# Latent attention scores: three products of 96 to 98 rows repacked into two of 128 rows and one of 34 rows that lies in another row half for each head of a pair

## The chip, the core and the metric

The kernel runs on one core of one Trainium2 chip. The metric is the device time of one execution in microseconds; the time before is the median of three runs. The engines are named as the profile names them: PE (TensorE, the matmuls; PEld is its weight load), DVE (VectorE), ACT (ScalarE), POOL (GpSimd) and SP (SyncE, which issues the DMAs).

## What is computed

A trunk of two layers works on 1024 latent tokens and 256 context tokens of width 1024. Layer 0 is attention with two head groups (8 grouped-query heads and 8 latent heads), layer 1 is recurrent. The change lies in the latent heads of layer 0. Cut from the reference:

```python
qa = (rms_norm(cq, q_norm_a) @ w_uq).reshape(bsz, t, MLA_HEADS, MLA_NOPE + MLA_ROPE)   # 64 + 32
kv = (rms_norm(ckv, kv_norm_a) @ w_ukv).reshape(bsz, t, MLA_HEADS, MLA_NOPE + MLA_V)   # 64 + 64
q_rope = apply_axial_rope(q_rope, rope_a); kr = apply_axial_rope(kr, rope_a)
qa = concatenate([q_nope, q_rope]); ka = concatenate([k_nope, broadcast_to(kr)])       # 96 each
sc = einsum('bqhgd,bkhd->bhgqk', qblk, k) * scale
p  = softmax(sc); o = einsum('bhgqk,bkhd->bqhgd', p, v)
```

Each head's key and query thus have 96 elements: 64 of its own, and 32 rotary ones, whose key part all heads share.

## The kernel before, in words

All matmuls of the scores take operands of the type float32r. To come near float32, every operand is split into a high part h and a low part l, and a product is the sum of three matmuls into one PSUM tile: hh, hl and lh.

`attention` (L594) is a generator that first runs beside the input projection and then alone. Its work is a list of 16 units: 8 of the grouped-query heads ("g"), then 8 of the latent heads ("m"). A unit is a pair of heads p and a part of the query tokens: S0 is 512 latent tokens and the 256 context tokens, S1 the other 512 latent tokens. A unit is worked off in steps `it`, one for each block of 128 keys: 10 steps for a segment of 512 queries, 2 for the 256 context queries (which see the context keys alone). So the latent heads have 4 x 2 x 10 steps of 512 columns and 4 x 2 steps of 256.

The main loop (L975) does for each step, in this order: `scores` of the next step (L792), `sums` of the step before (L830, softmax sums, on POOL and partly DVE), and after every second step `values` for both (L815, PSUM tile pv, 64 output columns for each of the two heads). `scores` computes 128 keys x 512 queries for head j = 0, then for j = 1, each in a PSUM tile "pb" of a ring of 3, and ACT takes exp of it into a tile "pt" of a ring of 11. For a latent head these are three matmuls (L808 to L810):

```python
self.mm(sp[:, :n], kh[0:98, ks], qh[0:98, j, o], True, False)
self.mm(sp[:, :n], kh[0:96, ks], ql[0:96, j, o], False, False)
self.mm(sp[:, :n], kl[0:96, ks], qh[0:96, j, o], False, True)
```

Rows 96 and 97 of kh are ones, those of qh the two bf16 terms of minus the row maximum.

Between the matmuls of `scores` the function `between` lets the generator `prep` of the next unit issue pieces: for a unit with base 0 first `prep_k_mla` (L688: three chunks of tokens, 256, 512 and 512; the key projection of both heads, split into kh and kl), then for all units `prep_q_mla` (L711: for each head and segment six projection matmuls, the rotary product with the table `tab` on DVE, and the split into qh and ql), then `prep_max` (L734: score matmuls of 128 queries against the keys in high parts alone, whose row maxima DVE takes, and the `bias` that writes them back as two rows). The PSUM tiles of `prep` ("ps") come from a ring of 4. Small work tiles "f" (L638, L722) are a ring of 3.

PE and DVE issue in the order in which the program is written there (a manual schedule, L943); ACT, POOL and SP in the order that a scheduler gives them. Every engine issues in its order.

The shared rotary part of the keys is made once in `project0` (`krb`, L396 to L430) and stored to DRAM as `d["kr"]`, 64 rows of high part (32 rows, then ones) and 64 rows of low part (32 rows, then zeros), from where `prep_k_mla` loads it under each head's 64 rows.

Of the kernel before, what the change touches and what calls it, by code (L numbers as in the profile page):

```python
# [17 lines left out]
P = 128  # L18
D = 1024
# [92 lines left out]
class Trunk:  # L112
# [202 lines left out]
    def project0(self, er, el, att):  # L315
# [84 lines left out]
        nc.gpsimd.tensor_copy(krb[:, :, 0, 96:128], one.rearrange("p (a b) -> p a b", a=4))  # L400

        def post_a(c):
# [15 lines left out]
            nc.gpsimd.tensor_copy(krb[:, :nt, 0, 64:96], kr)  # L418
# [175 lines left out]
    def attention(self, es):  # L594
# [12 lines left out]
        def kb_tile(first):  # L607
            return self.til(u0, [P, NTOK], F32R, "kb", bufs=2) if first else self.til(ap, [P, NTOK], F32R, "kb", bufs=6)
# [63 lines left out]
        def q_tiles(u):  # L672
            u["qh"], u["ql"] = (self.til(u0, [P, 2, 768], F32R, t, bufs=2) for t in ("qh", "ql"))
            return u["qh"], u["ql"]
# [13 lines left out]
        def prep_k_mla(u):  # L688
            p = u["p"]
            kh, kl = [], []  # L690
            for j in range(2):
                a, b = (kb_tile(p % 2 and j) for _ in range(2))
                nc.sync.dma_start(a.bitcast(F32)[64:128], d["kr"][0])
                nc.sync.dma_start(b.bitcast(F32)[64:96], d["kr"][1, 0:32])
                kh.append(a)
                kl.append(b)
            u["k"] = [(kh[0], kl[0]), (kh[1], kl[1])]
            wu, ck = M["wu"], M["ck"]
            ws = slice(p * P, (p + 1) * P)
            for t0, n in CH:  # L700
# [3 lines left out]
                nc.scalar.activation(kh[0][0:64, tk], acc[0:64, :n], AF.Copy)  # L704
                nc.vector.tensor_tensor(kl[0][0:64, tk], acc[0:64, :n], kh[0][0:64, tk], op=ALU.subtract)
                sc = self.til(ap, [P, 512], F32, "f", bufs=3)
                nc.scalar.copy(sc[0:64, :n], acc[64:128, :n])
                self.split(kh[1][0:64, tk], kl[1][0:64, tk], sc[0:64, :n], "v", "g")
                yield

        def prep_q_mla(u):  # L711
            qh, ql = q_tiles(u)
            wq, cq, tab = M["wq"], M["cq"], M["tab"]
            for j in range(2):
                h = 2 * u["p"] + j
                for t0, n in u["segs"]:
# [3 lines left out]
                    for k in range(2):  # L720
                        self.mm3(acc[:, :n], wq[:, k, 0, h], wq[:, k, 1, h], cq[:, k, 0, tk], cq[:, k, 1, tk], k == 0, k == 1)
                    qs = self.til(ap, [P, 512], F32, "f", bufs=3)  # L722
                    if t0 == 0:
                        nc.scalar.copy(qs[0:96, :n], acc[0:96, :n])
                    else:
                        lt = slice(t0 - NCTX, t0 - NCTX + n)
                        w = self.til(ap, [P, 512], F32, "f", bufs=3)
                        nc.vector.tensor_tensor(qs[0:96, :n], acc[0:96, :n], tab[0:96, lt], op=ALU.mult)
                        nc.vector.tensor_tensor(w[64:96, :n], acc[96:128, :n], tab[96:128, lt], op=ALU.mult)
                        nc.vector.tensor_tensor(qs[64:96, :n], qs[64:96, :n], w[64:96, :n], op=ALU.add)  # L730
                    self.split(qh[0:96, j, o], ql[0:96, j, o], qs[0:96, :n], "a", "g")
                    yield

        def prep_max(u):  # L734

            K, r0 = (P, 64) if u["kind"] == "g" else (96, 96)
            mt = u["ql"] if u["kind"] == "g" else u["qh"]
# [4 lines left out]
            def bias(j, t0, n):  # L742
                o = t0 - u["base"]
                pm = self.ps([P, 512])
                for i in range(n // P):
                    self.mm(pm[r0:r0 + 2, i * P:(i + 1) * P], nb[:, j, o // P + i, :], self.ident_bf, True, True)
                nc.scalar.activation(mt[r0:r0 + 2, j, o:o + n], pm[r0:r0 + 2, :n], AF.Copy)
# [44 lines left out]
        def scores(it):  # L792
# [6 lines left out]
            for j in range(2):  # L799
                if j:  # L800
                    yield
                sp = self.ps([P, 512], "pb")
                kh, kl = u["k"][j]
                if u["kind"] == "g":
                    self.mm(sp[:, :n], kh[:, ks], qh[:, j, o], True, False)
                    self.mm(sp[:, :n], kl[0:66, ks], ql[0:66, j, o], False, True)
                else:
                    self.mm(sp[:, :n], kh[0:98, ks], qh[0:98, j, o], True, False)  # L808
                    self.mm(sp[:, :n], kh[0:96, ks], ql[0:96, j, o], False, False)
                    self.mm(sp[:, :n], kl[0:96, ks], qh[0:96, j, o], False, True)  # L810
# [1430 lines left out]
```

## Time and profile before

| | |
|---|---|
| median of three runs | 1787.96 us (1785.87 to 1790.78) |
| the profiled execution, its own time | 1786.52 us |
| its span in the profile, first to last instruction | 1784.7 us |
| mean granted TensorE clock over the span | 0.960 of full speed |
| PE, PEld, DVE, ACT, POOL busy, share of the span | 91%, 67%, 66%, 42%, 45% |
| latent heads' steps, first and last score matmul | 608.8 us and 906.4 us after the span's start |

The profile has a page (busy shares, the span in slices, DMA queues, the chain that ended last, the costliest groups) and a trace that can be asked for a stretch. A matmul's shown duration contains its way through the array: matmuls overlap, so what one costs in a row of them is the distance from its start to the next start, not its duration. In a timeline, equal instructions that follow each other stand in one row with their count. An engine's idle time stands with what ended it.

### The profile page before, as it was taken

The numbers are of one execution on the slowest core, as the hardware profiler recorded it, in microseconds if no ns is written. First come the engines' busy times: TensorE is split into PE (matmuls) and PEld (weight loads), VectorE is DVE, ScalarE is ACT, GpSimd is POOL, SyncE is SP. The second block draws the span as 40 slices with busy tenths as digits, with TensorE's granted clock in tenths as the row PEclk, the third lists the DMA queues.
The fourth block names the chain that finished last, engine by engine and source line by source line (L and its number), as shares of the span: only waits on it lengthen the run. The fifth ranks groups of instructions, "written<-read, shape, count | busy, mean of one in ns | idle before, by whom it ended". The sixth has DMA issues, their size and how long they took to land.

```text
span 1784.7 us, 25505 instructions
## 1 busy us (share of the span) xinstructions
PE 1630.5 (91%) x9020; PEld 1195.9 (67%) x9020; DVE 1177.7 (66%) x2186; ACT 741.0 (42%) x1500; POOL 811.2 (45%) x727
## 2 busy tenths in 40 slices
PE   5999899989999999999899989988978995898996
PEld 2997766735555566666457876666856883798885
DVE  2657623247566857667847975889956894477787
ACT  2543401145545454444524344767643421233431
POOL 1432200067666678767643851332213794572131
PEclk9999999999999999999999999989989997899998
DMA  9243485164322101121333323333458538985543
GB/s 354 75 154 109 147 292 201 60 142 144 94 53 59 35 22 47 30 59 48 98 98 113 130 91 102 111 107 115 145 140 213 159 115 233 295 259 174 172 147 106
DMA packets 239931, 234.31 MB, mean 131 GB/s; under 512 B 61958, under 2 KB 188306, under 8 KB 237756
## 3 DMA queue, kind: packets, MB, share of 16 engines
q1 hardware_dynamic: 239804, 232.69, 42.8%
q8 instruction: 71, 1.16, 0.3%
q14 instruction: 56, 0.46, 0.1%
HBM read 162.97 MB, written 69.66 MB: 130 GB/s over the span
## 4 chain that ended last, share of the span: by engine, by line
PE 51%; DVE 18%; DMA 13%; issue 7%; ACT 6%; POOL 3%; SPq 2%; ACTq 0%; DVEq 0%; POOLq 0%
PE ps L88 34%; PE pb L88 10%; PE pv L88 7%; DMA wst<-in_att_w_in 2%; DVE f L88 2%; DMA wh<-in_rec_w_out 2%; DVE x L88 2%; DVE yc L88 2%; DVE lw L88 1%; DVE mx L88 1%; DMA qh<-d_q 1%; DMA d_xa<-WX 1%; DVE WX L88 1%; DVE r L88 1%; DVE lu L88 1%
## 5 line engine op out<-in xcount | busy, mean ns | idle before, releaser
L88 DVE TENSOR_REDUCE mx<-ps 128x1 f32<-128x512 f32 (+1 forms) x384 | 207.2, 593 | 155.8 <-PE ps L88 154.1
L88 POOL TENSOR_TENSOR accp<-accp,pt 128x512 f32<-128x512 f32 x202 | 266.0, 1338 | 62.0 <-ACT pt L88 60.4
L88 PE MATMUL ps<-h1h,wf 128*128 128x512 f32 (+1 forms) x864 | 270.5, 388 | 3.5 <-DVE tm L88 1.6
L88 ACT ACTIVATE pt<-pb 128x512 f32<-128x512 f32 (+1 forms) x352 | 194.2, 577 | 185.7 <-PE pb L88 178.0
L88 PE MATMUL pb<-qh,kb 96*128 96x512 f32 (+4 forms) x528 | 210.0, 412 | 5.2 <-ACT pt L88 4.6
L88 PEld LDWEIGHTS ps<-h1h,wf 128*128 128x128 f32 x864 | 161.1, 194 | 35.4 <-issue 3.7
L88 PE MATMUL ps<-h1l,wf 128*128 128x512 f32 (+1 forms) x432 | 163.7, 379 | 0.0
L88 PEld LDWEIGHTS pb<-qh,kb 128*128 128x128 f32 (+2 forms) x528 | 100.1, 191 | 92.6 <-issue 65.4
L88 PE MATMUL pb<-ql,kb 66*128 66x512 f32 (+3 forms) x352 | 137.5, 392 | 0.7 <-ACT ql L88 0.7
L88 PE MATMUL ps<-kb,qh 128*128 128x512 f32 (+3 forms) x416 | 121.7, 368 | 8.9 <-DVE mx L88 5.0
L88 POOL TENSOR_TENSOR accp<-pt,pt 128x512 f32<-128x512 f32 (+1 forms) x47 | 55.9, 1208 | 137.0 <-ACT pt L88 125.3
L88 PEld LDWEIGHTS ps<-kb,qh 128*128 128x128 f32 (+1 forms) x416 | 76.9, 191 | 44.8 <-DVE mx L88 12.8
L88 POOL TENSOR_TENSOR ml<-m,mh 128x512 fp32r<-128x512 f32 (+1 forms) x24 | 52.6, 2205 | 114.0 <-ACT mh L88 114.0
L88 DVE SCALAR_TENSOR_TENSOR yc<-xb,rT,yc 128x1283 f32<-128x1283 f32 (+1 forms) x48 | 84.1, 1759 | 24.5 <-ACT yc L88 24.1
L88 PEld LDWEIGHTS ps<-h1l,wf 128*128 128x128 f32 x432 | 83.9, 194 | 16.6 <-issue 3.6
L88 PE MATMUL ps<-w,mh 128*128 128x512 f32 x256 | 82.5, 404 | 3.4 <-ACT mh L88 3.4
L88 PE MATMUL pv<-pt,vm 128*64 128x512 f32 (+1 forms) x352 | 83.1, 586 | 1.6 <-DVE mo L88 1.6
L88 PE MATMUL pv<-pt,vgqa 128*64 128x512 f32 (+1 forms) x352 | 83.1, 593 | 1.0 <-DVE mo L88 1.0
L88 PE MATMUL ps<-wo,mh 128*128 128x512 f32 x256 | 82.1, 399 | 1.2 <-ACT mh L88 0.7
L88 PE MATMUL ps<-wh,hh 128*128 128x416 f32 (+2 forms) x240 | 82.8, 349 | 0.2 <-ACT hs L88 0.2
L88 PE MATMUL ps<-wh,hl 128*128 128x416 f32 (+2 forms) x240 | 81.7, 343 | 0.0
L88 PE MATMUL ps<-wl,hh 128*128 128x416 f32 (+2 forms) x240 | 81.5, 342 | 0.0
(373 smaller groups left out, 3706.0 us busy)
## 6 DMA issues: line engine op xcount, KB each, us to landing
modw<-in_mod_w SPq DMA_DIRECT2D x16, 1024.0 KB
wfs<-in_rec_w_in SPq DMA_DIRECT2D x22, 512.0 KB
modw<-in_mod_w SPq DMA_DIRECT2D x16, 512.0 KB
wst<-in_att_w_in SPq DMA_DIRECT2D x24, 256.0 KB
d_q<-qo SPq DMA_DIRECT2D x20, 256.0 KB
lx<-d_xl SPq DMA_DIRECT2D x8, 640.0 KB
d_w<-WX SPq DMA_DIRECT2D x20, 256.0 KB
W<-d_w SPq DMA_DIRECT2D x20, 256.0 KB
```

Source lines behind the costliest of these rows:

```text
L88: return fn(*args, **kw)
```

## The change

The same 290 products per query and key (98 + 96 + 96) are laid out as 128 + 128 + 34 rows. Of one head, the first matmul holds [kh of 64 rows; rotary kh; rotary kh] against [qh of 64; rotary qh; rotary ql]; the second holds kh and kl of the 64 rows against ql and qh, one above the other; the third holds 32 rows of the rotary kl and the two rows of ones against the rotary qh and the maximum. The third operand's keys ("kc") are loaded once for all heads, in rows 0 to 33 and again in rows 64 to 97; head 0 of a pair uses the upper half and head 1 the lower one, so the two third matmuls stand next to each other, in tiles of 64 rows. For that, `scores` opens the second head's PSUM tile before it ends the first's, and exp of the first head comes after the two.

Preparation: `prep_k_mla` makes four ACT copies and two DVE subtractions per chunk (before: two ACT copies, a DVE subtraction, a DVE cast, a POOL subtraction); `prep_q_mla` makes for a segment of 512 four ACT copies, four DVE operations and a POOL one (before: one, three, one), for the segment of 256 five ACT copies, one DVE and one POOL operation (before: two, none, one). Tiles: the ring pt goes from 11 to 10; the tiles of q have one buffer for S0 and one for S1 instead of a ring of two of equal size; the tiles of keys of even p get a pool of their own ("kx"), with the same reuse as before.

```diff
--- before.py
+++ after.py
@@ -397,7 +397,7 @@
         one = self.til(wka, [P, P], F32, "ones", bufs=1)
         nc.gpsimd.memset(one, 1.0)
         nc.gpsimd.memset(krb.bitcast(F32), 0.0)
-        nc.gpsimd.tensor_copy(krb[:, :, 0, 96:128], one.rearrange("p (a b) -> p a b", a=4))
+        nc.gpsimd.tensor_copy(krb[:, :, 1, 96:128], one.rearrange("p (a b) -> p a b", a=4))
 
         def post_a(c):
             t0, n = CH[c]
@@ -415,7 +415,7 @@
                     nc.gpsimd.tensor_tensor(s5(u)[:, :, :, h], s5(kr)[:, :, :, 1 - h], s5(sin32[:, tt])[:, :, :, h], op=ALU.mult)
                 nc.gpsimd.tensor_tensor(v, v, u, op=ALU.add)
                 kr = v
-            nc.gpsimd.tensor_copy(krb[:, :nt, 0, 64:96], kr)
+            nc.gpsimd.tensor_copy(krb[:, :nt, 0, 64:128].rearrange("p t (r e) -> p t r e", r=2), kr.unsqueeze(2).broadcast_to([P, nt, 2, 32]))
             nc.gpsimd.tensor_tensor(krb[:, :nt, 1, 64:96], kr, krb[:, :nt, 0, 64:96], op=ALU.subtract)
             for a, b, q in ((0, 256, 0), (256, 384, 4)):
                 nc.gpsimd.tensor_tensor(r[:, :nt, a:b], r[:, :nt, a:b], rs[:, q:q + nt].unsqueeze(2).broadcast_to([P, nt, b - a]), op=ALU.mult)
@@ -604,8 +604,10 @@
                 for segs in (S0, S1):
                     units.append(dict(kind=kind, p=p, segs=segs, f=p + (4 if kind == "g" else 0), base=min(x[0] for x in segs), i=len(units)))
 
-        def kb_tile(first):
-            return self.til(u0, [P, NTOK], F32R, "kb", bufs=2) if first else self.til(ap, [P, NTOK], F32R, "kb", bufs=6)
+        def kb_tile(first, even=False):
+            if even:
+                return self.til(kx, [P, NTOK], F32R, "kx", bufs=4)
+            return self.til(u0 if first else ap, [P, NTOK], F32R, "kb", bufs=2)
 
         gk = []
 
@@ -670,7 +672,8 @@
                 yield
 
         def q_tiles(u):
-            u["qh"], u["ql"] = (self.til(u0, [P, 2, 768], F32R, t, bufs=2) for t in ("qh", "ql"))
+            n = sum(x[1] for x in u["segs"])
+            u["qh"], u["ql"] = (self.til(u0, [P, 2, n], F32R, f"{t}{n}", bufs=1) for t in ("qh", "ql"))
             return u["qh"], u["ql"]
 
         def prep_q_gqa(u):
@@ -687,54 +690,66 @@
 
         def prep_k_mla(u):
             p = u["p"]
-            kh, kl = [], []
+            ka, kb = [], []
             for j in range(2):
-                a, b = (kb_tile(p % 2 and j) for _ in range(2))
+                a, b = (kb_tile(p % 2 and j, p % 2 == 0) for _ in range(2))
                 nc.sync.dma_start(a.bitcast(F32)[64:128], d["kr"][0])
-                nc.sync.dma_start(b.bitcast(F32)[64:96], d["kr"][1, 0:32])
-                kh.append(a)
-                kl.append(b)
-            u["k"] = [(kh[0], kl[0]), (kh[1], kl[1])]
+                ka.append(a)
+                kb.append(b)
+            u["k"] = [(ka[0], kb[0]), (ka[1], kb[1])]
+            if "kc" not in M:
+                kc = M["kc"] = self.til(ap, [P, NTOK], F32R, "kc", bufs=1)
+                for j in range(2):
+                    nc.sync.dma_start(kc.bitcast(F32)[64 * j:64 * j + 64], d["kr"][1])
             wu, ck = M["wu"], M["ck"]
             ws = slice(p * P, (p + 1) * P)
             for t0, n in CH:
                 acc = self.ps([P, 512])
                 tk = slice(t0, t0 + n)
                 self.mm3(acc[:, :n], wu[:, 0, 0, ws], wu[:, 0, 1, ws], ck[:, 0, tk], ck[:, 1, tk], True, True)
-                nc.scalar.activation(kh[0][0:64, tk], acc[0:64, :n], AF.Copy)
-                nc.vector.tensor_tensor(kl[0][0:64, tk], acc[0:64, :n], kh[0][0:64, tk], op=ALU.subtract)
-                sc = self.til(ap, [P, 512], F32, "f", bufs=3)
-                nc.scalar.copy(sc[0:64, :n], acc[64:128, :n])
-                self.split(kh[1][0:64, tk], kl[1][0:64, tk], sc[0:64, :n], "v", "g")
+                nc.scalar.activation(ka[0][0:64, tk], acc[0:64, :n], AF.Copy)
+                nc.vector.tensor_tensor(kb[0][64:128, tk], acc[0:64, :n], ka[0][0:64, tk], op=ALU.subtract)
+                nc.scalar.activation(kb[1][64:128, tk], acc[64:128, :n], AF.Copy)
+                nc.vector.tensor_tensor(kb[1][0:64, tk], acc[64:128, :n], kb[1][64:128, tk], op=ALU.subtract)
+                nc.scalar.activation(kb[0][0:64, tk], acc[0:64, :n], AF.Copy)
+                nc.scalar.activation(ka[1][0:64, tk], acc[64:128, :n], AF.Copy)
                 yield
 
         def prep_q_mla(u):
+
+
             qh, ql = q_tiles(u)
+            qc = u["qc"] = self.til(ap, [P, sum(x[1] for x in u["segs"])], F32R, f"qc{u['base'] // 768}", bufs=1)
             wq, cq, tab = M["wq"], M["cq"], M["tab"]
             for j in range(2):
                 h = 2 * u["p"] + j
+                bh, bl = (slice(64, 128), slice(0, 64)) if j == 0 else (slice(0, 64), slice(64, 128))
                 for t0, n in u["segs"]:
                     tk = slice(t0, t0 + n)
                     o = slice(t0 - u["base"], t0 - u["base"] + n)
                     acc = self.ps([P, 512])
                     for k in range(2):
                         self.mm3(acc[:, :n], wq[:, k, 0, h], wq[:, k, 1, h], cq[:, k, 0, tk], cq[:, k, 1, tk], k == 0, k == 1)
+                    nc.scalar.activation(qh[0:64, j, o], acc[0:64, :n], AF.Copy)
+                    nc.vector.tensor_tensor(ql[bl, j, o], acc[0:64, :n], qh[0:64, j, o], op=ALU.subtract)
+                    nc.scalar.activation(ql[bh, j, o], acc[0:64, :n], AF.Copy)
                     qs = self.til(ap, [P, 512], F32, "f", bufs=3)
                     if t0 == 0:
-                        nc.scalar.copy(qs[0:96, :n], acc[0:96, :n])
+                        nc.scalar.copy(qs[64:96, :n], acc[64:96, :n])
                     else:
                         lt = slice(t0 - NCTX, t0 - NCTX + n)
                         w = self.til(ap, [P, 512], F32, "f", bufs=3)
-                        nc.vector.tensor_tensor(qs[0:96, :n], acc[0:96, :n], tab[0:96, lt], op=ALU.mult)
+                        nc.vector.tensor_tensor(qs[64:96, :n], acc[64:96, :n], tab[64:96, lt], op=ALU.mult)
                         nc.vector.tensor_tensor(w[64:96, :n], acc[96:128, :n], tab[96:128, lt], op=ALU.mult)
                         nc.vector.tensor_tensor(qs[64:96, :n], qs[64:96, :n], w[64:96, :n], op=ALU.add)
-                    self.split(qh[0:96, j, o], ql[0:96, j, o], qs[0:96, :n], "a", "g")
+                    nc.scalar.activation(qh[64:96, j, o], qs[64:96, :n], AF.Copy)
+                    nc.gpsimd.tensor_tensor(qh[96:128, j, o], qs[64:96, :n], qh[64:96, j, o], op=ALU.subtract)
+                    nc.scalar.activation(qc[64 * j:64 * j + 32, o], qs[64:96, :n], AF.Copy)
                     yield
 
         def prep_max(u):
 
-            K, r0 = (P, 64) if u["kind"] == "g" else (96, 96)
-            mt = u["ql"] if u["kind"] == "g" else u["qh"]
+            K = P if u["kind"] == "g" else 96
             mx = self.til(u0, [P, 8, 3], F32, "mx", bufs=2)
             m8 = self.til(u0, [P, 2, 6, 2], F32, "m8", bufs=2)
             nb = self.til(u0, [P, 2, 6, 2], BF16, "nb", bufs=2)
@@ -742,9 +757,14 @@
             def bias(j, t0, n):
                 o = t0 - u["base"]
                 pm = self.ps([P, 512])
+                if u["kind"] == "g":
+                    r0, dst = 64, u["ql"][64:66, j, o:o + n]
+                else:
+                    r0 = 32 + 64 * j
+                    dst = u["qc"][r0:r0 + 2, o:o + n]
                 for i in range(n // P):
                     self.mm(pm[r0:r0 + 2, i * P:(i + 1) * P], nb[:, j, o // P + i, :], self.ident_bf, True, True)
-                nc.scalar.activation(mt[r0:r0 + 2, j, o:o + n], pm[r0:r0 + 2, :n], AF.Copy)
+                nc.scalar.activation(dst, pm[r0:r0 + 2, :n], AF.Copy)
 
             for t0, n in u["segs"]:
                 if t0 == 0:
@@ -796,21 +816,34 @@
             qh, ql = u["qh"], u["ql"]
             scale = 64 ** -0.5 if u["kind"] == "g" else 96 ** -0.5
             it["pt"] = []
-            for j in range(2):
-                if j:
-                    yield
-                sp = self.ps([P, 512], "pb")
-                kh, kl = u["k"][j]
-                if u["kind"] == "g":
+
+            def exp(sp):
+                pt = self.til(ap, [P, 512], F32, "pt", bufs=10)
+                nc.scalar.activation(pt[:, :n], sp[:, :n], AF.Exp, scale=scale)
+                it["pt"].append(pt)
+
+            if u["kind"] == "g":
+                for j in range(2):
+                    if j:
+                        yield
+                    sp = self.ps([P, 512], "pb")
+                    kh, kl = u["k"][j]
                     self.mm(sp[:, :n], kh[:, ks], qh[:, j, o], True, False)
                     self.mm(sp[:, :n], kl[0:66, ks], ql[0:66, j, o], False, True)
-                else:
-                    self.mm(sp[:, :n], kh[0:98, ks], qh[0:98, j, o], True, False)
-                    self.mm(sp[:, :n], kh[0:96, ks], ql[0:96, j, o], False, False)
-                    self.mm(sp[:, :n], kl[0:96, ks], qh[0:96, j, o], False, True)
-                pt = self.til(ap, [P, 512], F32, "pt", bufs=11)
-                nc.scalar.activation(pt[:, :n], sp[:, :n], AF.Exp, scale=scale)
-                it["pt"].append(pt)
+                    exp(sp)
+                return
+            kc, qc = M["kc"], u["qc"]
+            sp = self.ps([P, 512], "pb")
+            for k, q in zip(u["k"][0], (qh, ql)):
+                self.mm(sp[:, :n], k[:, ks], q[:, 0, o], q is qh, False)
+            yield
+            s1 = self.ps([P, 512], "pb")
+            self.mm(sp[:, :n], kc[0:34, ks], qc[0:34, o], False, True)
+            self.mm(s1[:, :n], kc[64:98, ks], qc[64:98, o], True, False)
+            exp(sp)
+            for k, q in zip(u["k"][1], (qh, ql)):
+                self.mm(s1[:, :n], k[:, ks], q[:, 1, o], False, q is ql)
+            exp(s1)
 
         def values(it):
             u, t0, n, kb, nkb = it["u"], it["t0"], it["n"], it["kb"], it["nkb"]
...
```

(Left out: the opening and closing of the pool "kx", and names of tiles that the end of the function reuses.)

How the order moves on PE, in the place of one step of 512 columns of the latent heads (pair p = 2, between the key projection and the first maxima; names: pb score tiles, qh/ql/qc query parts, kb/kx/kc key tiles). Before:

```order
L88 MATMUL pb_1732_7004<-qh_1599_6531,kb_1489_6126 128x512
L88 MATMUL pb_1732_7004<-ql_1600_6532,kb_1489_6126 128x512
L88 MATMUL pb_1732_7004<-qh_1599_6531,kb_1490_6127 128x512
L88 MATMUL pb_1734_7010<-qh_1599_6531,kb_1491_6130 128x512
L88 MATMUL pb_1734_7010<-ql_1600_6532,kb_1491_6130 128x512
L88 MATMUL pb_1734_7010<-qh_1599_6531,kb_1492_6131 128x512
```

The same place in the changed kernel:

```order
L88 MATMUL pb_1729_7073<-qh512_1597_6576,kb_1488_6153 128x512
L88 MATMUL pb_1729_7073<-ql512_1598_6577,kb_1489_6154 128x512
L88 MATMUL pb_1729_7073<-qc1_1599_6578,kc_1285_5402 128x512
L88 MATMUL pb_1730_7076<-qc1_1599_6578,kc_1285_5402 128x512
L88 MATMUL pb_1730_7076<-qh512_1597_6576,kb_1490_6156 128x512
L88 MATMUL pb_1730_7076<-ql512_1598_6577,kb_1491_6157 128x512
```

The count stays at six; the third and the fourth are now the pair of 34 rows, with two full ones ahead and two behind.

On ACT, where the keys and queries of pair p = 2 are prepared (kb/kx keys, qh/ql queries, f work tiles, pt exponentials). Before, from the second key copy of the first chunk on:

```order
L88 COPY f_1702_6890<-ps_1701_6884 64x256
L88 ACTIVATE kb_1697_6876<-ps_1705_6904 64x512
L88 ACTIVATE pt_1708_6918<-pb_1707_6914 128x512
L88 COPY f_1704_6900<-ps_1703_6894 64x512
L88 COPY f_1706_6910<-ps_1705_6904 64x512
L88 ACTIVATE pt_1717_6953<-pb_1716_6949 128x512
L88 COPY f_1715_6943<-ps_1714_6936 96x256
L88 ACTIVATE pt_1724_6984<-pb_1723_6980 128x512
```

In the changed kernel, from the exponential that answers to the first of these on:

```order
L88 ACTIVATE pt_1704_6970<-pb_1702_6963 128x512
L88 ACTIVATE kx_1698_6931<-ps_1700_6943 64x512
L88 ACTIVATE qh768_1705_6972<-ps_1708_6975 64x512
L88 ACTIVATE qh768_1705_6972<-ps_1711_6993 64x256
L88 ACTIVATE kx_1696_6928<-ps_1700_6943 64x512
L88 ACTIVATE kx_1697_6930<-ps_1700_6943 64x512
L88 ACTIVATE kx_1698_6931<-ps_1701_6953 64x512
L88 ACTIVATE kx_1696_6928<-ps_1701_6953 64x512
L88 ACTIVATE kx_1697_6930<-ps_1701_6953 64x512
L88 ACTIVATE qh768_1705_6972<-ps_1714_7013 64x512
L88 ACTIVATE ql768_1706_6973<-ps_1708_6975 64x512
L88 ACTIVATE qh768_1705_6972<-ps_1717_7031 64x256
```

Where two copies stood between two exponentials, eleven stand now ahead of the next one.

## Rows read from the trace of the kernel before

**Rows 1.** Busy time by stage of the latent heads; columns: us, PE, PEld, DVE, ACT, POOL (instructions), clock, DMA.

```profile
726.00:801.20 75.20, 74.95 (x351) 46.50 (x351) 49.78 (x103) 35.52 (x67) 55.17 (x45) 1.00 0.16 41
...
876.30:906.80 30.50, 27.10 (x105) 14.55 (x105) 22.93 (x19) 13.54 (x22) 18.69 (x12) 0.89 0.29 89
```

**Rows 2.** All waits of PE itself, 600 to 850 us; columns: total us, times, longest us.

```profile
PE pb L88 <- ACT qh L88: 0.3, 2, 0.2
```

**Rows 3.** Score matmuls of the latent heads by shape, whole span; busy us, mean ns, idle before.

```profile
L88 PE MATMUL pb<-qh,kb 98*128 98x512 f32 x160 | 69.5, 434 | 0.5 <-ACT qh L88 0.3
...
L88 PE MATMUL pb<-qh,kb 98*128 98x256 f32 x16 | 4.9, 309 | 0.0
```

**Rows 4.** Timeline of PE, score matmuls of 512 and of 256 columns; start us, us.

```profile
737.48 0.63 PE L88 MATMUL pb<-qh,kb 96*128 96x512 f32 x2
737.95 0.39 PE L88 MATMUL pb<-ql,kb 96*128 96x512 f32 x1
738.18 0.39 PE L88 MATMUL pb<-qh,kb 96*128 96x512 f32 x1
...
719.14 0.40 PE L88 MATMUL pb<-qh,kb 96*128 96x256 f32 x2
719.38 0.28 PE L88 MATMUL pb<-ql,kb 96*128 96x256 f32 x1
719.50 0.28 PE L88 MATMUL pb<-qh,kb 96*128 96x256 f32 x1
```

**Rows 5.** Timeline of PE in layer 1: a single 16-row matmul among full ones.

```profile
1334.50 0.39 PE L88 MATMUL ps<-maskr,negi 128*128 128x512 f32 x1
1334.82 0.49 PE L88 MATMUL ps<-dec 16*128 16x512 f32 x1
1335.24 0.50 PE L88 MATMUL ps<-h1l,wf 128*128 128x512 f32 x1
1335.58 0.63 PE L88 MATMUL ps<-h1h,wf 128*128 128x512 f32 x2
```

**Rows 6.** Timeline of PE, float32: full matmuls; two of 32 rows in two row groups (L1095).

```profile
1238.89 1.88 PE L88 MATMUL ps<-lx,gw 128*128 128x512 f32 x4
...
1624.47 1.13 PE L88 MATMUL ps<-grows,sel 32*128 32x512 f32 x4
1625.53 0.22 PE L88 MATMUL ps<-zz,Tu 32*32 32x32 f32 x2
```

**Rows 7.** Timeline of PE around the half-width pv matmuls of the latent heads.

```profile
708.66 1.94 PE L88 MATMUL pv<-pt,vm 128*64 128x512 f32 x8
710.53 0.50 PE L88 MATMUL pb<-qh,kb 98*128 98x512 f32 x1
710.87 0.40 PE L88 MATMUL pb<-ql,kb 96*128 96x512 f32 x1
```

**Rows 8.** The preparation stretch of pair 2, columns as in rows 1.

```profile
726.00:738.40 12.40, 12.40 (x61) 8.70 (x61) 7.11 (x12) 7.42 (x16) 6.44 (x6) 1.00 0.08 21
```

**Rows 9.** Timeline of ACT at the end of a preparation.

```profile
813.94 0.41 ACT L88 ACTIVATE qh<-f 96x256 fp32r<-96x256 f32 x1
814.26 1.55 ACT L88 ACTIVATE pt<-pb 128x512 f32<-128x512 f32 x3
```

**Rows 10.** The preparation of pair 0: timeline, then its window, columns as in rows 1.

```profile
584.28 4.71 DVE L88 TENSOR_TENSOR f<-f,f 32x512 f32<-32x512 f32 x1
...
584.72 2.51 POOL L88 TENSOR_TENSOR accp<-pt,pt 128x512 f32<-128x512 f32 x2
...
587.19 1.26 POOL L88 TENSOR_TENSOR accp<-accp,pt 128x512 f32<-128x512 f32 x1
...
589.77 1.09 PE L88 MATMUL ps<-kb,qh 96*128 96x512 f32 x2 [3.27 <-DVE mx L88]
...
575.00:600.00 25.00, 21.62 (x92) 12.68 (x92) 17.80 (x30) 12.12 (x24) 19.21 (x17) 0.93 0.05 12
```

**Rows 11.** ACT's exponentials in the latent heads, 619 to 913 us; idle before, releasers.

```profile
L88 ACT ACTIVATE pt<-pb 128x512 f32<-128x512 f32 x155 | 90.0, 595 | 87.4 <-PE pb L88 82.7 <-PE ps L88 2.8
```

More of the change, by code (lines that the diff above doesn't have):

```diff
@@ L922, in attention @@
         ap = self.ap = self.pool(ea, "attn", 2)
+        ek = ExitStack()
+        kx = self.pool(ek, "attk")
         load_gk(1)
@@ L1001, in attention @@
                 em.close()
-                kt = [self.til(ap, [P, NTOK], F32R, "kb", bufs=6)[:, 0:D] for _ in range(4)]
+                ek.close()
+                kx = self.pool(ea, "attl")
+                kt = [self.til(kx, [P, D], F32R, "kt", bufs=4) for _ in range(4)]
                 wo = self.w_out(I["att_w_out"][0], [x.bitcast(F32) for x in kt[:2]])
@@ L1010, in attention @@
                     pass
-                spare = lambda t: self.til(u0, [P, 2, 768], F32R, t, bufs=2).rearrange("p a b -> p (a b)")[:, 0:D].rearrange("p (k t) -> p k t", t=P)
+                spare = lambda t: self.til(u0, [P, 2, 768], F32R, t + "768", bufs=1).rearrange("p a b -> p (a b)")[:, 0:D].rearrange("p (k t) -> p k t", t=P)
                 ml, ml1 = spare("qh"), spare("ql")
```

## The prediction

> **What bounds the kernel now.** I read the stages first. In the latent heads PE is busy 74.95 of 75.20 us in the period of one pair of heads, DVE 49.78, ACT 35.52, POOL 55.17, at full granted clock [rows 1]; the reader sees an engine that never stops. The waits say the same: from 600 to 850 us PE itself stood still for 0.3 us in all [rows 2]. So in this stage a microsecond more or less on PE is one on the end, until another engine falls behind. Only the last unit is looser (27.10 of 30.50 us) [rows 1].
>
> Then I read the price of a matmul there, from start to start. Score matmuls of 512 columns start at 737.48, (second of the row), 737.95 and 738.18: three distances in 0.70 us, 0.233 us each; of 256 columns three in 0.36, 0.12 each [rows 4]. There are 80 steps of 512 columns (160 matmuls over two heads) and 8 of 256 [rows 3].
>
> **The change on PE.** The number of matmuls stays six per step. What can be gained is that the two of 34 rows run side by side: one slot of 0.233 us per step of 512, 80 x 0.233 + 8 x 0.12 = 19.6 us in all.
>
> What it can cost is the way into and out of the small row tiles, twice per step. Latent scores have none now, but layer 1 has lone float32r matmuls of 16 rows among full ones [rows 5]. The full one ahead starts at 1334.50, the small one at 1334.82, the next full one at 1335.24 and the one after it at 1335.58: 0.32 + 0.42 + 0.34 = 1.08 us for three distances that take 0.70 between full matmuls. The round trip costs 0.38 us. The first matmul after half-width column tiles shows the same late second start, 710.53 to 710.87, 0.34 [rows 7].
>
> Do the two small ones share a slot? Four full float32 records of 512 columns take 1.88 us of which the last lasts 0.59, so 1.29 for three distances, 0.43 each; the four records of two 32-row matmuls in two row groups take 1.13, so 0.54 from first to last start where 1.29 would be serial [rows 6]. They run in pairs; I take the pair as one slot and 0.01 us.
>
> So from the second full matmul of head 0 to the second of head 1, four distances of 0.233 = 0.93 us become 1.08 + 0.01: **0.16 us more per step of 512**. In a step of 256, 4 x 0.12 = 0.48 become 3 x 0.12 + 0.38 + 0.01 = 0.75, 0.27 more. Sum: 80 x 0.16 + 8 x 0.27 = **15.0 us more**. Row tiles of 64 do not occur in this stage before the change, so bounds: below, no cost of switching at all (minus 19.6 us); above, the small ones one after the other (0.21 more per step of 512, 0.1 of 256: 15.0 + 17.6 = 32.6). I take the 16-row rows because they are the same kind of matmul among the same neighbours.
>
> Against this stands a rule of the Trainium skill. Its page "TensorE: Matmul & The Clock Gate", section Part 3, gives a pack of tiles the time of one matmul plus about 4 ns for each further tile, and no price for getting in or out; the sum by it would be the 19.6 us of gain. The 32-row rows agree with the sharing, the 16-row rows do not agree that it is free to enter. The page "TensorEngine Tiling (Array Packing)", Key Properties, says that a change of the tiling mode drains the engine, with no figure; what hangs on it is the 0.38 us, and the trace agrees.
>
> **The change in preparation.** For a unit with base 0 ACT makes, by the code, per chunk of keys two copies more (two chunks of 512, one of 256) and per query segment three more (two of 512, two of 256): 10 of 512 and 8 of 256. Back to back an ACT operation takes (1.55 - 0.59) / 2 = 0.48 us for 512 columns and 814.26 - 813.94 = 0.32 for 256 [rows 9]: 4.8 + 2.6 = 7.4 us more. The stretch from the first key projection to the first maxima is 12.40 us long, with PE busy throughout and ACT 7.42 [rows 8]. ACT would need 14.8 us in it. In the order eleven copies now stand ahead of an exponential, and the PSUM ring of four is freed by the last copy of a chunk; so PE, which ran on, waits for ring tiles late in the stretch. The excess is 14.8 - 12.4 = 2.4 us, and ACT can begin only after the first projection (three matmuls of 256, 0.36 us by [rows 4]) and waits for DVE inside: I take 3 us for each of pairs 1, 2 and 3, **9 us**. From below 0 (all of it slides under later matmuls), from above the whole 7.4 each, 22. Pair 0 is prepared beside the last grouped-query unit and already has such a stop, PE 3.27 us behind DVE [rows 10]: no change taken, plus or minus 5. Units of S1 get six more copies, 2.9 us, with the ring never full and ACT idle half the time [rows 1]: 0.
>
> **Edits costed at nothing.** DVE gets six subtractions more per pair and has 25 us idle; POOL loses three subtractions per pair and is no bound [rows 1]; without that cover they would be costs of the same size. The ring pt with 10 tiles: ACT's exponentials waited for matmuls alone, never for POOL to free a tile [rows 11]; one tile less would show there first. The key loads change by a few rows per pair plus two loads of 64 rows once, on SP, a unit ahead of use. The pools keep the same reuse. The wider copy in `krb` is one POOL operation of 64 instead of 32 elements per token tile, three times.
>
> **Sum.** The profiled execution took 1786.52 us. 1786.5 + 15.0 + 9 = 1810.5; the median of the runs shown lies 1.4 above that execution, so **1812 us**. This forecast's own range is 1798 (no stop in preparation, pair 0's stop gone: 1788 + 15 - 5) to 1820 (5 us per pair and 0.02 more per step).
>
> **The rivals.**
> A, faster: half-row tiles are entered for nothing. Then 1788 - 19.6 + 0 to 9 = 1768 to 1777. For it: the sharing is in the trace [rows 6], and no row shows a 64-row tile in these surroundings. Against it: both the 16-row tiles [rows 5] and the half-width ones [rows 7] pay. It decides where the round trip costs less than the slot saved, 0.22 us of the 0.38.
> B, the pair does not run side by side, because it streams float32r into two banks that are both in use: 15.0 + 17.6 + 9, 1830. Against it [rows 6].
> C, preparation becomes the bound. In pair 0 a DVE addition of 32 x 512 took 4.71 us while POOL worked through three additions, PE stood for 3.27 us, and the granted clock of the 25 us fell to 0.93 [rows 10], 25 x 0.07 = 1.7 us lost: 5 us per stop. In the changed order POOL waits for an ACT copy ahead of its additions and then has them all ready, so this could happen in pairs 1 to 3 too, on top of the 3 us each: 1812 + 15 = 1827.
> D, no difference: switches at half the price (0.19 us the round trip: 80 steps win 0.03, 8 lose 0.08, about minus 2 us) and preparation hidden: 1784 to 1790.
>
> **How the numbers follow.** Forecast 0.66, C 0.15, A 0.09, B 0.06, D 0.04. What a measurement can tell from no change is about 0.3%, 5.4 us. Faster 0.09 (A), within it 0.04 (D), slower 0.87. The range 1795 to 1830 holds the forecast, C and the lower half of B; it leaves out A, D and the rest, under 0.2.
>
> **What would show it.** Right: in the latent heads the two 34-row matmuls start within 0.01 us of each other, 0.32 us after the one ahead, the next full one 0.42 us later and its follower 0.34 after it; a pair's period grows from 75.2 to about 82 us (3.2 + 0.5 from 20 steps of 512 and 2 of 256, 3 from preparation); PE waits in the preparation for ACT on "ps". Wrong: distances of 0.23 around the pair (A), the small ones 0.21 apart or more (B), a period over 84 us with long DVE additions (C), or a stage that is not shifted as a whole, because PE was not its bound.

## The result

The changed kernel took 1868.62 us in the median of four runs (1866.07 to 1870.72), the kernel before on the same chip 1789.32 (1785.87 to 1790.78): a ratio of 1.0436, 95% interval 1.0415 to 1.0458. Slower was forecast, but by 24 us and not by 79; the time lies far outside the range and outside every rival.

The stages of the changed kernel, columns as in rows 1. The first two rows are pairs 2 and 3 of the heads, the third is the whole latent stage, from the first key projection of pair 0 to the last score matmul:

```profile
758.60:854.00 95.40, 87.37 (x351) 44.56 (x350) 55.46 (x110) 48.41 (x91) 51.87 (x42) 0.91 0.11 29
854.00:949.00 95.00, 86.22 (x340) 43.39 (x338) 62.41 (x114) 54.42 (x97) 52.54 (x41) 0.91 0.19 57
...
576.50:980.80 404.30, 369.74 (x1470) 186.36 (x1469) 251.12 (x460) 212.83 (x391) 224.51 (x176) 0.91 0.14 39
```

The same whole stage of the kernel before:

```profile
573.70:906.80 333.10, 324.12 (x1470) 195.80 (x1469) 234.52 (x435) 159.94 (x293) 236.99 (x188) 0.98 0.18 50
```

The span grew by 1864.2 - 1784.7 = 79.5 us, and 71.2 of it lie in this stage. A pair that took 75.20 us with PE busy for 74.95 at full clock [rows 1] takes 95.40, with PE still for 8.03 us and a granted clock of 0.91. The page shows the clock as well. It cuts the span into 40 slices, and the stage is the 13th to the 21st: four of them (the 16th, 18th, 20th and 21st) stand at 8, where the page of before has nines throughout the stage:

```profile
PEclk9999999999999998989888999998988997999998
```

Where PE stands, 650 to 950 us, as in rows 2 (total us, times, longest). Before, the waits of a stretch of this stage came to 0.3 us in all [rows 2]:

```profile
PE ps L88 <- DVE f L88: 8.5, 6, 2.0
PE ps L88 <- DVE mx L88: 7.4, 6, 1.7
PE ps L88 <- ACT kb L88: 5.3, 4, 1.7
PE ps L88 <- ACT kx L88: 2.7, 2, 1.7
PE pv L88 <- DVE mo L88: 1.3, 1, 1.3
```

All but the last line (one wait, at the end of pair 3) are waits for a tile of the preparation's ring "ps", 18 in number. One pair of heads has six of them, here those of pair 2 in the timeline of PE (start us, us, the idle time before it and what ended it in brackets):

```profile
765.99 1.66 PE L88 MATMUL ps<-cq,wuq 128*128 128x512 f32 x6 [1.74 <-ACT kx L88]
768.56 0.98 PE L88 MATMUL ps<-cq,wuq 128*128 128x256 f32 x6 [0.92 <-ACT kx L88]
...
776.21 0.47 PE L88 MATMUL ps<-kx,qh 96*128 96x512 f32 x1 [0.86 <-DVE f L88]
778.34 0.39 PE L88 MATMUL ps<-kx,qh 96*128 96x256 f32 x1 [1.66 <-DVE mx L88]
...
820.09 0.77 PE L88 MATMUL ps<-kx,qh 96*128 96x512 f32 x1 [1.96 <-DVE f L88]
822.53 1.18 PE L88 MATMUL ps<-kx,qh 96*128 96x512 f32 x2 [0.81 <-DVE mx L88]
```

Two in the key projection (2.66 us), two at the first maxima of unit S0 (2.52), two at those of S1 (2.77): 7.95 of the 8.03 us. After the second group the clock goes to the lower of its two levels (1.2 GHz, a granted clock of 0.50); in the third it goes there at the end of the first stop (1.00 up to 819.5 us, 0.50 from 819.8 on). It stays there while PE works on, in the first row without a break, in the second from 822.53 on:

```profile
778.80:785.60 6.80, 6.80 (x18) 3.08 (x18) 2.82 (x6) 2.77 (x6) 6.49 (x7) 0.50 0.01 1
822.00:830.00 8.00, 7.47 (x18) 3.20 (x20) 4.21 (x8) 2.12 (x4) 4.63 (x4) 0.50 0.00 1
```

The first group is different: from 758.6 to 778.0 us, over both stops of the key projection, the clock is at 1.00.

**The sum over the stage.** PE not busy: 404.30 - 369.74 = 34.56 against 8.98, 25.6 us more. Clock: 0.09 of 404.30 against 0.02 of 333.10 not granted, 29.7 us more. The way through the row tiles, as forecast: 15.0. Together 70.3 of the 71.2; since the clock is given to 0.01, its term is good to about 4 us. The 8.3 us outside the stage (2.8 ahead of it, 5.5 behind it) stay open.

**The chain that holds the ring.** VectorE and ScalarE in unit S1 of pair 2, just ahead of the stop that ends at 820.09:

```profile
811.10 0.68 DVE L88 TENSOR_TENSOR ql<-ps,qh 64x512 fp32r<-64x512 f32 x1 [2.10 <-ACT qh L88]
812.51 1.42 DVE L88 TENSOR_TENSOR f<-ps,mlat 32x512 f32<-32x512 f32 x2 [0.72 <-ACT ql L88]
813.96 1.50 DVE L88 TENSOR_TENSOR f<-f,f 32x512 f32<-32x512 f32 x1
815.49 1.67 DVE L88 TENSOR_TENSOR accv<-pt,pt 128x512 f32<-128x512 f32 x1
817.19 0.68 DVE L88 TENSOR_TENSOR ql<-ps,qh 64x512 fp32r<-64x512 f32 x1
818.53 1.42 DVE L88 TENSOR_TENSOR f<-ps,mlat 32x512 f32<-32x512 f32 x2 [0.66 <-ACT ql L88]
```

```profile
810.47 0.59 ACT L88 ACTIVATE qh<-ps 64x512 fp32r<-64x512 f32 x1 [0.73 <-PE ps L88]
811.81 0.59 ACT L88 ACTIVATE ql<-ps 64x512 fp32r<-64x512 f32 x1 [0.75 <-DVE ql L88]
...
817.91 0.59 ACT L88 ACTIVATE ql<-ps 64x512 fp32r<-64x512 f32 x1 [1.13 <-DVE ql L88]
```

The two engines take turns on one PSUM tile: ACT copies qh, DVE subtracts, ACT copies the second time (`ql[bh]`), and only then does DVE begin the rotary products, the last readers of the tile. While ACT makes the second copy DVE is idle, for 0.72 and 0.66 us: the copy's 0.59 us and 0.03 to 0.11 us at each change-over. So PE waits for "DVE f", the products, and they for ACT's copy. Before the change, DVE's products followed the matmuls directly, in the same unit:

```profile
766.55 1.42 DVE L88 TENSOR_TENSOR f<-ps,mlat 96x512 f32<-96x512 f32 x2 [1.17 <-PE ps L88]
```

From DVE's first operation on the first tile to the end of its products on the second it now takes 8.85 us (811.10 to 819.95), before 5.45 (766.55 to 772.00). The 3.40 more are two subtractions (1.36), the two waits for ACT's second copy (1.38) and the softmax sum "accv" of 1.67 us, where it took 0.69 (0.98); the addition between takes 1.50 instead of 1.82.

The section "PSUM bank collisions raise a hardware error" of the Trainium skill's page "PSUM — Partial Sum Buffer" says that two engines must not touch the same bank in the same group of 32 rows at one time, reads included. By that the second copy and the subtraction, both of rows 0 to 63, have to take turns; the trace agrees that they do (the first copy comes ahead of the subtraction in any case, which needs its result). The products read rows 64 to 127 and wait all the same, so this kernel takes turns by whole tile. Whether turns by group of rows would do was not tried.

### The profile page after: what moved, and what is told of

It reads as the page before. It is cut to its first block, busy times and chain, and to the rows that moved or that the text cites. A ratio compares the mean times of both kernels' runs of the same rounds, so it can differ in the third digit from the quotient of the medians.

```text
span 1864.2 us, 25592 instructions
## 1 busy us (share of the span) xinstructions
PE 1677.1 (90%) x9020; PEld 1187.9 (64%) x9020; DVE 1192.9 (64%) x2210; ACT 793.1 (43%) x1596; POOL 796.2 (43%) x715
## 4 chain that ended last, share of the span: by engine, by line
PE 45%; DVE 23%; DMA 13%; ACT 9%; issue 6%; POOL 2%; SPq 2%; DVEq 0%; ACTq 0%; POOLq 0%
PE ps L88 27%; PE pb L88 11%; PE pv L88 8%; DVE f L88 2%; DVE yc L88 2%; DMA wst<-in_att_w_in 2%; DMA wh<-in_rec_w_out 2%; DVE x L88 2%; DVE ia L88 1%; DVE r L88 1%; DMA d_xa<-WX 1%; DVE WX L88 1%; DVE lw L88 1%; DVE itmp L88 1%; DVE mx L88 1%
## 5 line engine op out<-in xcount | busy, mean ns | idle before, releaser
L88 PE MATMUL pb<-qh,kb 128*128 128x512 f32 (+1 forms) x264 | 118.0, 449 | 3.3 <-ACT pt L88 3.3
L88 PE MATMUL ps<-kb,qh 128*128 128x512 f32 (+3 forms) x312 | 96.7, 386 | 14.3 <-DVE mx L88 6.6
L88 PE MATMUL pb<-ql,kb 66*128 66x512 f32 (+3 forms) x264 | 104.6, 398 | 0.9 <-ACT ql L88 0.9
L88 PEld LDWEIGHTS pb<-qh,kb 128*128 128x128 f32 x264 | 51.0, 193 | 73.3 <-issue 60.4
L88 PE MATMUL pv<-pt,vm 128*64 128x512 f32 (+1 forms) x352 | 95.5, 663 | 1.3 <-DVE mo L88 1.3
L88 PEld LDWEIGHTS ps<-kb,qh 128*128 128x128 f32 (+1 forms) x312 | 59.4, 198 | 45.6 <-DVE mx L88 12.4
```

Source lines behind the costliest of these rows:

```text
L88: return fn(*args, **kw)
```

## The experiments

Theory 1 after the result: the 15 us on PE are real, and the rest is the turn-taking in the preparation, which stops PE and thereby lowers its clock. The rivals: the row tiles cost much more than the 15 us or lower the clock themselves, or it is the number of ScalarE copies. The first four kernels ran together (before: 1787.82 us in the median of seven runs).

**full_third: no row tiles, preparation as changed.** The two 34-row matmuls become two of 98 rows over zero-padded operands, on the whole array.

```diff
-            self.mm(sp[:, :n], kc[0:34, ks], qc[0:34, o], False, True)
-            self.mm(s1[:, :n], kc[64:98, ks], qc[64:98, o], True, False)
+            self.mm(sp[:, :n], kc[0][0:98, ks], qc[0:98, o], False, True)
+            self.mm(s1[:, :n], kc[1][0:98, ks], qc[0:98, o], True, False)
```

> The changed kernel with the third matmul of either head over 98 rows (a second key tile, zeros in the other head's rows, the ring pt at 8 to make room), so that PE never enters a row tile; all preparation as changed. Theory 1 (the trace of the changed kernel: of 20.0 us more per pair of heads, the row-tile pairs make 3.7 and stops of PE in preparation with the low clock after them 16.3): 1868.6 - 15 = 1854 us, between 1847 and 1860, and the low-clock stretches stay. Theory 2 (the row tiles themselves bring the clock down): most of the 79 us come back, 1790 to 1810, and the granted clock of the latent heads is 1.0.

1846.12 us, ratio 1.0324 (1.030 to 1.0349). Most of the loss stands, 58 of 79 us, so the rival falls. It is 22.5 us faster than the changed kernel, a little more than theory 1 allowed for. In the profiles the stage itself is 14.0 us shorter (404.30 to 390.30), near the 15 of the row tiles; where the rest comes from stays open. The stage still has them, and the lower clock with them, without any row tile:

```profile
575.90:966.20 390.30, 351.97 (x1470) 205.78 (x1469) 251.39 (x459) 211.37 (x390) 225.11 (x176) 0.91 0.14 41
```

**reorder_q: one line moved.** The second ScalarE copy is issued behind the rotary products; every copy is still made.

```diff
-                    nc.scalar.activation(ql[bh, j, o], acc[0:64, :n], AF.Copy)
...
+                    nc.scalar.activation(ql[bh, j, o], acc[0:64, :n], AF.Copy)
                     nc.scalar.activation(qh[64:96, j, o], qs[64:96, :n], AF.Copy)
```

> The changed kernel with one line moved: in the query preparation the second copy of the high part is issued after the rotary products instead of before them; every operation stays. Theory 1a (the stops come from ACT and DVE taking turns on one PSUM tile: DVE's products wait for an ACT copy that stands behind exponentials): the S1 units' stops go and with them their low clock, some 8 us per pair, and a part of the others: 1815 to 1845. Theory 1b (the stops come from the number of ACT copies): no change, 1860 to 1875.

1821.44 us, ratio 1.0181 (1.0146 to 1.0216): 47 us from the place of one line. DVE's products now follow its subtraction at once, in the same unit:

```profile
786.69 0.68 DVE L88 TENSOR_TENSOR ql<-ps,qh 64x512 fp32r<-64x512 f32 x1 [2.10 <-ACT qh L88]
787.41 1.42 DVE L88 TENSOR_TENSOR f<-ps,mlat 32x512 f32<-32x512 f32 x2
788.86 0.68 DVE L88 TENSOR_TENSOR f<-f,f 32x512 f32<-32x512 f32 x1
```

The stretch that took 8.85 us takes 6.68 (786.69 to 793.37). Of the 2.17 less, 1.38 are the two waits; the rest is the addition behind the first products, which takes 0.68 us instead of 1.50: it comes earlier, and is not beside POOL's additions for its whole length, as it is in the changed kernel. PE's stop at the maxima of S1 is 0.43 us instead of 2.77, and the pair runs at full clock; the stops of the key projection are still there (1.75 and 0.91). The profile is that of the fastest of the four runs, 1813.20 us:

```profile
794.16 0.50 PE L88 MATMUL ps<-kx,qh 96*128 96x512 f32 x1 [0.43 <-ACT ql L88]
...
738.80:823.30 84.50, 80.17 (x351) 41.59 (x350) 53.21 (x109) 48.20 (x91) 51.84 (x42) 1.00 0.11 32
```

PE's busy time falls by 87.37 - 80.17 = 7.2 us with the same matmuls: that is what the lower clock cost in a pair. Its idle time falls by only 8.03 - 4.33 = 3.7.

**sbuf_dup: as many copies, none of them a further read of PSUM.** The repeated copies, one per query segment and two per key chunk, read the SBUF tile that the first copy wrote.

```diff
-                    nc.scalar.activation(ql[bh, j, o], acc[0:64, :n], AF.Copy)
+                    nc.scalar.activation(ql[bh, j, o], qh[0:64, j, o], AF.Copy)
```

> The changed kernel with the repeated copies of high parts (one per query segment, two per chunk of keys) taken from the first copy in SBUF instead of from the PSUM tile; as many ACT operations as before. Theory 1a: PSUM tiles come free earlier, 1805 to 1835. Theory 1b: no change, 1860 to 1875.

1826.41 us, ratio 1.0206 (1.0163 to 1.0248): ACT's work is unchanged and 42 us are gone. So the number of copies is not what costs most. The stops of the key projection are still there, 1.42 and 1.49 us in pair 2.

**dma_dup: the repeated copies as transfers.**

```diff
-                    nc.scalar.activation(ql[bh, j, o], acc[0:64, :n], AF.Copy)
+                    nc.sync.dma_start(ql.bitcast(F32)[bh, j, o], qh.bitcast(F32)[0:64, j, o])
```

> The changed kernel with the same repeated copies made by DMAs from SBUF to SBUF instead of by ACT: 10 ACT operations fewer per unit with base 0, 2 fewer in the others. Theory 1a and 1b alike: most stops go, 1803 to 1825; what is left over 1789 + 15 is what the copies did not cause. If it stays over 1845, the stops have another cause (the DVE work or POOL).

1812.05 us, ratio 1.0135 (1.0111 to 1.0159). 24 us above before, of which 15 should be row tiles; the next kernel tested that. It is 14 us faster than sbuf_dup: that is what the copies cost as work of ACT. The stops of the key projection shrink to 0.44 us.

```profile
740.70:822.60 81.90, 79.76 (x350) 41.74 (x349) 53.51 (x109) 42.95 (x79) 52.08 (x42) 1.00 0.19 49
```

**dma_full: dma_dup and full_third together**, with a probability ring of 8. This and the next two ran beside a before of 1789.59 us (11 runs).

> The changed kernel with the repeated copies as transfers (as in the run dma_dup, 1812.05 us) and also with both pair matmuls spread over 98 rows (as in full_third), so neither row tiles nor turn-taking are left. The probability ring is 8 instead of 10. Theory 1 (a round trip into the row tiles costs 15.0 us of PE time and that is on the path also when nothing stops PE): 1797 us, 1792 to 1802, a pair of heads shorter by 3 to 4 us than in dma_dup. Rival (what dma_dup has left over the kernel before is still preparation, the tiles are nearly free once PE does not stop): 1807 to 1814, the same period as dma_dup.

1800.83 us, ratio 1.0076 (1.0053 to 1.0098). PE's busy time in a pair without a dip of the clock:

```profile
648.80:727.80 79.00, 75.94 (x351) 46.17 (x350) 53.04 (x110) 42.44 (x79) 52.59 (x43) 1.00 0.20 51
```

79.76 - 75.94 = 3.8 us per pair of heads for the row tiles, 15.3 for four. That is the term of the prediction. The whole gained less, 11 us by the medians: with PE faster, its idle time in the pair went from 2.14 to 3.06 us, at the maxima (1.25 after 0.99) and at two places that dma_dup did not stop at. The median lies near the upper end of theory 1's range (1792 to 1802) and below the rival's (from 1807 on); the period, 2.9 us shorter than in dma_dup, rules the rival out too.

**turn_alone: the turns alone, in the kernel before.** No row tile, no other key layout; the probability ring is 10 instead of 11.

```diff
+                    da = self.til(ap, [P, 512], F32, "da", bufs=1)
+                    nc.scalar.activation(da[0:64, :n], acc[0:64, :n], AF.Copy)
+                    nc.vector.tensor_tensor(da[64:128, :n], acc[0:64, :n], da[0:64, :n], op=ALU.subtract)
+                    nc.scalar.activation(da[0:64, :n], acc[0:64, :n], AF.Copy)
                     qs = self.til(ap, [P, 512], F32, "f", bufs=3)
```

> The kernel before, all matmuls as they were, with the turns alone added to the query preparation: ahead of the rotary products a ScalarE copy of rows 0 to 63 of the accumulator, a VectorE subtraction that reads it, and a second ScalarE copy into the same scratch rows; the results are not used. The probability ring is 10 instead of 11. Theory 1 (the chain of turns on one accumulator holds the ring of four, PE stops about 3 us and then 7 to 10 us at the lower clock level, per preparation): 20 to 45 us more than before, 1808 to 1833, with PE stops on the VectorE products' tile in both halves of each pair and stretches at a granted clock near 0.5. Rival (the turns hurt only together with the row tiles or with the longer key preparation): within 8 us of before, 1785 to 1796, clock 0.96.

1836.89 us, ratio 1.0268 (1.0242 to 1.0294): 47 us, just over what theory 1 gave. The pattern is that of the changed kernel, in a kernel whose score matmuls are untouched:

```profile
769.64 0.77 PE L88 MATMUL ps<-kb,qh 96*128 96x512 f32 x1 [2.48 <-DVE f L88]
772.26 0.58 PE L88 MATMUL ps<-kb,qh 96*128 96x256 f32 x1 [1.86 <-DVE mx L88]
811.78 0.47 PE L88 MATMUL ps<-kb,qh 96*128 96x512 f32 x1 [1.67 <-DVE f L88]
814.02 1.18 PE L88 MATMUL ps<-kb,qh 96*128 96x512 f32 x2 [1.06 <-DVE mx L88]
...
754.40:843.10 88.70, 81.49 (x350) 49.40 (x349) 54.08 (x109) 41.73 (x79) 55.26 (x45) 0.90 0.12 34
```

**after_fill: useless matmuls where PE would stop.** In the changed kernel, ahead of the matmuls for the maxima at which it stops (`nf` is 4, 7, 8 or 4).

```diff
+                                fl, kf = self.ps([P, 512], "pb"), u["k"][0][0]
+                                for _ in range(nf):
+                                    self.mm(fl, kf[:, 0:P], kf[:, 0:512], True, True)
```

> The changed kernel with useless work added: in every latent unit 4 and 7 (first units of a pair) or 8 and 4 (second units) extra full-height matmuls of 512 columns into a spare score accumulator that nothing reads, just ahead of the matmuls for the maxima at which the changed kernel stops for 0.86 and 1.66 us, and 1.96 and 0.81 us. 23 per pair of heads by 0.233 us is 5.4 us, as much as the stops they replace (5.3 us). Theory 1 (the short stops are what lowers the clock, and its lower level then costs about 8 us per pair of heads on top): the granted clock stays at the upper level there, the stops shrink, the period falls from 95 to about 87 us, and the time to 1830 to 1848 although PE does more. Rival (the clock falls for another reason, or the accumulators are held just as long whatever PE does): nothing gained, 1863 to 1872, or the extra matmuls add up to 22 us, 1875 to 1890, with the stretches at the lower level still there.

1842.43 us beside a before of 1789.28, ratio 1.0291 (1.0244 to 1.0339): 26 us faster than the changed kernel, with 92 matmuls more, as theory 1 said. PE works where it stood, and its clock stays up. What is left of its waits in the pair are the two stops of the key projection, and they do not lower the clock:

```profile
PE ps L88 <- ACT kx L88: 2.6, 2, 1.7
...
752.90:841.00 88.10, 85.22 (x374) 45.87 (x373) 54.14 (x110) 48.31 (x91) 52.09 (x42) 1.00 0.11 31
```

So the stops at the maxima lower the clock, and in this case the clock cost about as much as all stops together (29.7 against 25.6 us in the sum above).

**pair_edge: an attempt at a faster version.** dma_dup, with the 34-row pair moved to the border of the step that faces `values`, so that one trip out of the full-array mode serves two steps.

```diff
+            if it["i"] % 2:
+                pair(True)
+                full(0, s0, False)
...
+            else:
+                full(0, s0, True)
+                yield
+                full(1, s1, True)
+                yield
+                pair(False)
```

> dma_dup with the pair of 34 rows moved beside the 64-column value matmuls: in the step ahead of them the pair closes both sums as the last score matmuls, in the step behind them it opens both sums as the first ones; two exponentials then come together. Per two steps there is one run of pair, values, pair instead of three separate trips. If a change from row tiles to column tiles costs nothing beyond one entry and one exit: 44 runs less two trips of 0.38 us, 33 us less than dma_dup, 1779, below the kernel before. If such a change costs as much as an exit and an entry (0.38): nothing is saved, 1808 to 1816. If half: 1795. A rival mishap: the exponentials of two sums at once come late for the ring of three accumulators and PE waits on them, over 1820.

1798.68 us, ratio 1.006 (1.0038 to 1.0082): 13 us less than dma_dup, near the half-price case. The timeline of PE shows the price of each border:

```profile
761.80 0.49 PE L88 MATMUL pb<-qc,kc 34*128 34x512 f32 x2
762.23 1.94 PE L88 MATMUL pv<-pt,vm 128*64 128x512 f32 x8
764.09 0.50 PE L88 MATMUL pb<-qc,kc 34*128 34x512 f32 x2
764.53 0.50 PE L88 MATMUL pb<-qh,kb 128*128 128x512 f32 x1
764.87 0.40 PE L88 MATMUL pb<-ql,kb 128*128 128x512 f32 x1
...
730.70:808.50 77.80, 75.20 (x351) 42.18 (x350) 51.70 (x109) 41.62 (x79) 52.23 (x42) 1.00 0.20 52
```

From the pair to the column tiles 0.43 us, as to a full matmul; PE busy 79.76 - 75.20 = 4.6 us less per pair of heads, 0.41 per two steps (11 of them), where two saved round trips would be 0.76. Even so PE is busy for 75.20 us per pair and was for 74.95 before [rows 1]: shared this far, the row tiles give back about what they cost and no more. No version tried beats the kernel before.

## Why the prediction was wrong

**What bounds the kernel: right.** The 71.2 us by which the latent stage grew, all of them time in which PE stood or worked longer, came through to the end (79.5 us).

**The change on PE, 15.0 us: right, and by its own distances.** Where the clock is at its upper level, two full matmuls, the pair and two full ones:

```profile
800.60 0.50 PE L88 MATMUL pb<-qh,kb 128*128 128x512 f32 x1
800.94 0.40 PE L88 MATMUL pb<-ql,kb 128*128 128x512 f32 x1
801.27 0.50 PE L88 MATMUL pb<-qc,kc 34*128 34x512 f32 x2
801.70 0.50 PE L88 MATMUL pb<-qh,kb 128*128 128x512 f32 x1
802.03 0.40 PE L88 MATMUL pb<-ql,kb 128*128 128x512 f32 x1
```

0.33, 0.43 and 0.33 us, where 0.32, 0.42 and 0.34 were read off a 16-row matmul of another layer [rows 5]; the two of the pair share one slot. In 4 of the 88 steps, one in each pair of heads, the second starts about 0.45 us after the first, some 1.8 us in all; its weight load waits there for ACT's copy of the row maximum into the query rows "qc":

```profile
803.79 0.18 PEld L88 LDWEIGHTS pb<-qc,kc 34*128 34x128 f32 x1 [0.27 <-ACT qc L88]
```

Between dma_dup and dma_full the term measured 15.3 us. Rivals A and B fall with it: the tiles are not entered for nothing, and the pair is not serial. The Trainium skill's "TensorE: Matmul & The Clock Gate", Part 3, is right on the pack by this trace, and its span without a price for the borders is what made rival A; "TensorEngine Tiling (Array Packing)", Key Properties, names the drain without a size; the round trip cost 0.38 us here.

**The preparation: this is the step that failed.** The prediction counted ACT's copies against a stretch of the projection and took 3 us for pairs 1 to 3, and for the six copies more of S1, "with the ring never full and ACT idle half the time: 0". For the projection itself the 3 us were near: PE stops there for 1.74 + 0.92 = 2.66, and the copies as work of ACT cost 14 us (sbuf_dup against dma_dup) where 9 were forecast. But the copies were priced as busy time of one engine, and what they are is links in a chain of two engines over one accumulator. Each further read in the middle of that chain adds its own duration to the time that the tile is held (0.59 us for the copy, 0.68 for the subtraction, and the change-overs), however idle both engines are. So the ring of four gave no free tile at the maxima of both units, and PE stood for 2.52 and 2.77 us per pair where the prediction has nothing. The evidence stood in the diff: the second copy is written between DVE's subtraction and DVE's products. sbuf_dup shows the count to be the wrong price (same copies, 42 us less), reorder_q the place to be the right one (47 us), turn_alone that it needs nothing else of the change (47 us with a chain that has a subtraction and two copies more).

**The clock: left to a rival and too small there.** Rival C had the kind right, a stop in preparation after which the clock falls, and priced it from rows 10 at 5 us for one stop per pair in pairs 1 to 3, 1827 us. There were two such places in each of these pairs, and each cost some 2.6 us of standing and 7.2 / 2 = 3.6 of lower clock. In pair 0 the preparation of S0 came out within the "plus or minus 5" (PE stands for 4.75 us where it stood for 3.27 [rows 10]); but its S1, put at nothing like the others, stops PE for 3.47 us, and from its first key projection to that of pair 1 it takes 87.2 us where it took 77.2. C's own cause, a DVE addition of several microseconds beside POOL, did not come: the additions in S1 take 1.50 and 1.77 us, and in the kernel before the two at the same place take 1.82 and 1.70. A smaller part of the delay is of C's kind, the 0.82 us by which reorder_q shortens the first of them.

**Edits costed at nothing.** DVE's subtractions and POOL's relief were covered as said, as busy time; as a link in the chain the subtraction was not free. The probability ring of 10 held ACT up once in the stage (2.35 us behind POOL's "accp", at 606 us), and PE did not stop for it. Of the signs given for being wrong, C's came true by half: the period over 84 us, without the long DVE additions that were to go with it.

## What to carry to other kernels

When a further instruction reads a PSUM tile that another engine also reads, price the time for which the tile is held, the waits of one engine for the other included, against the depth of the ring, and not only the busy time of the engine; and issue last what nobody waits for. Where PE is the bound, a stop of two or three microseconds can cost twice its length or more: at the maxima the lower clock behind it cost 3.6 us for each 2.6 of standing, in the key projection nothing. Matmuls packed into small row tiles among full ones have to save more than the border costs: here 0.38 us per trip, against 0.233 saved.

## What had not been expected of the hardware

That in the changed kernel stops of at most 2 us let the clock fall for several microseconds of unbroken work, so that 92 matmuls whose results nobody reads make a kernel 26 us faster. And that going straight from row tiles to column tiles costs as much as going to the full array (0.43 us from start to start in both cases), so that trips can be merged only in part: 0.41 us saved of 0.76.
